# RMSNorm with repeated rows on one NeuronCore: wide squares and reductions, roots on GpSimd, and copies shared with GpSimd

## The chip, the cores and the metric

The kernel runs on one NeuronCore of a Trainium2 chip. The metric is the device time of one execution in microseconds (us), and smaller is better. Four parts of the core matter here: ScalarE (ACT in the profile), VectorE (DVE), GpSimd (POOL), and SyncE (SP), which computes nothing but issues transfers to the core's 16 DMA engines. TensorE does no work in this kernel.

## What is computed

The input `x` has 8 x 512 = 4096 rows of 2048 float32 values. Each row is divided by its root mean square, multiplied elementwise by `gamma`, and written twice, in two neighbouring rows of the output. So 33.6 MB are read and 67.1 MB are written.

```python
x_rep = np.repeat(x, 2, axis=1)
rms = np.sqrt((x_rep ** 2).mean(axis=-1, keepdims=True) + 1e-6)
return (x_rep / rms * gamma[None, None, :]).astype(np.float32)
```

## The kernel before

**Tiles.** The 4096 rows are cut into 8 tiles of 128 partitions x K = 4 rows. A tile `y` in SBUF has 8 row slots of 2048 values in each partition, 64 KB. The load puts the four input rows into slots 4 to 7 (`K * (R - 1) + k`, with R = 2). The result of row k goes to slot 2k, and its copy to slot 2k + 1. So the output overwrites the input row by row, and the whole tile is stored in one piece of 8.4 MB (L55 to L59). The pool `rows` has three such buffers (L39): tile 3 takes the buffer of tile 0, tile 4 that of tile 1, and so on. A load into a buffer has to wait until the store that reads this buffer has landed.

**Work on one row.** ScalarE squares the row and sums it in one pass, with the squares themselves thrown away into PSUM (L64, `accum_out`), and takes the root of the mean (L68). VectorE takes the reciprocal (L73) and computes x times this number times gamma in one instruction, `scalar_tensor_tensor` (L74). It has two tensors as inputs: the row and `gamma_b`, which holds gamma in all 128 partitions.

**Work on one tile** (`compute`, L83). Four times the row work; then ScalarE copies the results of rows 0 and 1 into their second slots and VectorE does so for rows 2 and 3 (L81). Then the store is issued.

**What sets the order.** The schedule is written by hand: each engine works through its instructions in program order. All loads and stores stand in one queue, that of SyncE, and SyncE issues them strictly in this order: load 0 (in two halves), load 1, load 2, store 0, store 1, store 2, load 3, load 4, load 5, store 3, store 4, load 6, load 7, store 5, store 6, store 7 (L91, L99, L100 and the loop at L106 with `loads_after`). Each store waits for its tile's copies, each later load for the store of the tile that had its buffer. While SyncE waits for one of them, nothing that stands behind it can be issued.

**At the start** gamma is fetched in seven pieces on ScalarE's own queue into partition 0 of `gamma_b` (L95), and GpSimd spreads it over the partitions (L96). GpSimd does nothing else.

Of the kernel before, what the change touches and what calls it, by code (L numbers as in the profile page):

```python
# [1 line left out]

# [4 lines left out]


@with_exitstack
def kernel(  # L10
    ctx: ExitStack,
    tc: tile.TileContext,
    x: bass.AP,
    gamma: bass.AP,
    out: bass.AP,
):
    nc = tc.nc
    P = nc.NUM_PARTITIONS
    f32 = mybir.dt.float32
    Act = mybir.ActivationFunctionType  # L20
    Alu = mybir.AluOpType

    B, S, D = x.shape
    Bo, So, Do = out.shape
    R = So // S
    assert R == 2 and D == Do and B == Bo and So == S * R
    eps = 1e-6
    inv_d = 1.0 / float(D)


    K = 4
    N = B * S
    assert N % (P * K) == 0
    ntiles = N // (P * K)
    x_t = x.rearrange("b s d -> (b s) d").rearrange("(n p k) d -> n p k d", p=P, k=K)
    out_t = out.rearrange("b s d -> (b s) d").rearrange("(n p j) d -> n p (j d)", p=P, j=K * R)

    singles = ctx.enter_context(tc.tile_pool(name="singles", bufs=1))
    rows = ctx.enter_context(tc.tile_pool(name="rows", bufs=3))  # L39
    junk = ctx.enter_context(tc.tile_pool(name="junk", bufs=1, space=bass.MemoryType.PSUM))  # L40
    small = ctx.enter_context(tc.tile_pool(name="small", bufs=8))

    ys = []

    def load(i, eng, parts=1):


        y = rows.tile([P, K * R, D], f32, name="y")
        step = K // parts
        for k in range(0, K, step):  # L50
            at = K * (R - 1) + k
            eng.dma_start(out=y[:, at : at + step, :], in_=x_t[i, :, k : k + step, :])
        ys.append(y)

    def store(i, k0, k1):  # L55
        nc.sync.dma_start(  # L56
            out=out_t[i, :, R * k0 * D : R * k1 * D],
            in_=ys[i][:, R * k0 : R * k1, :].rearrange("p j d -> p (j d)"),
        )  # L59

    def square(i, k):
        sq = junk.tile([P, D], f32, name="sq")
        ss = small.tile([P, 1], f32, name="ss")
        nc.scalar.activation(  # L64
            out=sq[:], in_=ys[i][:, K * (R - 1) + k, :], func=Act.Square, accum_out=ss[:]
        )
        rms = small.tile([P, 1], f32, name="rms")
        nc.scalar.activation(out=rms[:], in_=ss[:], func=Act.Sqrt, scale=inv_d, bias=eps_t[:])  # L68
        return rms

    def scale(i, k, rms):
        rstd = small.tile([P, 1], f32, name="rstd")
        nc.vector.reciprocal(out=rstd[:], in_=rms[:])  # L73
        nc.vector.scalar_tensor_tensor(  # L74
            out=ys[i][:, R * k, :], in0=ys[i][:, K * (R - 1) + k, :], scalar=rstd[:], in1=gamma_b[:],
            op0=Alu.mult, op1=Alu.mult,
        )

    def repeat(i, k0, k1, copy):
        y_r = ys[i].rearrange("p (k r) d -> p k r d", r=R)  # L80
        copy(out=y_r[:, k0:k1, 1, :], in_=y_r[:, k0:k1, 0, :])  # L81

    def compute(i):  # L83
        for k in range(K):
            scale(i, k, square(i, k))
        repeat(i, 0, K // 2, nc.scalar.copy)
        repeat(i, K // 2, K, nc.vector.tensor_copy)


    ctx.enter_context(tc.manual_schedule())  # L90
    load(0, nc.sync, parts=2)  # L91
    gamma_b = singles.tile([P, D], f32, name="gamma_b")
    cuts = [0, *range(D // 4, D + 1, D // 8)]
    for c0, c1 in zip(cuts, cuts[1:]):
        nc.scalar.dma_start(out=gamma_b[0:1, c0:c1], in_=gamma[c0:c1].partition_broadcast(1))  # L95
    nc.gpsimd.partition_broadcast(out_ap=gamma_b[:], in_ap=gamma_b[0:1, :])  # L96
    eps_t = singles.tile([P, 1], f32, name="eps_t")
    nc.vector.memset(eps_t, eps)  # L98
    load(1, nc.sync)  # L99
    load(2, nc.sync)  # L100

    assert ntiles == 8
    loads_after = {2: (3, 4, 5), 4: (6, 7)}
    for i in range(ntiles):  # L106
        compute(i)
        store(i, 0, K)
        for j in loads_after.get(i, ()):
            load(j, nc.sync)  # L110


# [1 line left out]
_INS = ['x', 'gamma']  # L114
_OUTS = [((8, 1024, 2048), 'float32')]


# [23 lines left out]
```

## Time and profile before

| | |
|---|---|
| median of 3 runs | 239.39 us (239.35 to 239.60) |
| the profiled execution: its time, its span | 239.72 us, 237.9 us |
| VectorE busy | 96.5 us in 73 instructions (41% of the span) |
| ScalarE busy | 101.0 us in 106 instructions (42%) |
| GpSimd busy | 2.5 us in 5 instructions (1%) |
| moved by DMA | 100.69 MB, 423 GB/s over the span |

The span runs from the first to the last instruction of the profiled execution. The execution's own time is 1.8 us longer, for what lies around the span. "Busy" of an engine counts its computing instructions; waiting and the issuing of transfers do not count. The profile names an instruction by its source line, so "L74" is line 74 of the code above. In the strips with 40 digits each digit stands for 5.9 us and gives the busy share in tenths, with 9 for 90% or more.

### The profile page before, as it was taken

Reading aid. Unit: us, or ns where it says so; the run is one execution under the profiler, and the core shown is the slowest. Engines: PE = TensorE matmul, PEld = TensorE weight load, DVE = VectorE, ACT = ScalarE, POOL = GpSimd, SP = SyncE. Lnnn points to the kernel's source line nnn. Section 1 sums busy time; section 2 is a strip of 40 time slices with the busy share of each in tenths; the row PEclk is TensorE's granted clock in tenths of the full one; section 3 lists DMA queues with packets and bytes.
Section 4 is the critical chain, followed back from the end, with each engine's and each line's share of the span. In section 5 each row is a group of like instructions: output and inputs, shape, how many; then the busy total and the mean of one; then the engine's idle time right before and its main releaser. Section 6 shows DMA issues by size and latency. Waiting matters only on the chain.

```text
span 237.9 us, 287 instructions
## 1 busy us (share of the span) xinstructions
DVE 96.5 (41%) x73; ACT 101.0 (42%) x106; POOL 2.5 (1%) x5
## 2 busy tenths in 40 slices
DVE  0049999960000000059999960000199990000000
ACT  2697999900000000099999920000599960000000
POOL 0030000000000000000000000000000000000000
DMA  7999998989899998999998999989998989999994
GB/s 265 436 446 441 441 441 353 530 353 496 386 452 430 397 485 353 441 441 441 441 518 364 464 419 430 452 369 430 435 518 364 518 364 485 397 452 430 408 474 176
DMA packets 2464, 100.69 MB, mean 423 GB/s; under 512 B 279, under 2 KB 285, under 8 KB 286
## 3 DMA queue, kind: packets, MB, share of 16 engines
q1 hardware_dynamic: 2448, 100.66, 98.5%
q14 instruction: 2, 0.02, 0.0%
q10 hardware_dynamic: 14, 0.01, 0.0%
HBM read 33.56 MB, written 67.11 MB: 423 GB/s over the span
## 4 chain that ended last, share of the span: by engine, by line
DMA 58%; ACT 12%; DVE 9%; issue 1%; POOLq 1%; ACTq 1%; SPq 0%
DMA y<-in_x_dram 33%; DMA out_dram<-y 21%; ACT sq L64 8%; DVE y L74 7%; DMA gamma_b<-in_gamma_dram 4%; ACT y L81 3%; DVE y L81 2%; ACT rms L68 1%; POOLq L136 1%; ACTq L95 1%; DVE rstd L73 0%; POOLq L96 0%; SPq L56 0%
## 5 line engine op out<-in xcount | busy, mean ns | idle before, releaser
L64 ACT ACTIVATE sq<-y 128x2048 f32<-128x2048 f32 x32 | 59.7, 1865 | 87.8 <-DMA y<-in_x_dram 87.8
L74 DVE SCALAR_TENSOR_TENSOR y<-y,rstd,gamma_b 128x2048 f32<-128x2048 f32 x32 | 75.3, 2352 | 4.1 <-POOL gamma_b L96 3.0
L73 DVE RECIPROCAL rstd<-rms 128x1 f32<-128x1 f32 x32 | 5.0, 158 | 94.6 <-ACT rms L68 94.3
L81 ACT COPY y<-y 128x4096 f32<-128x4096 f32 x8 | 28.7, 3590 | 1.4 <-DVE y L74 1.4
L81 DVE COPY y<-y 128x4096 f32<-128x4096 f32 x8 | 18.3, 2294 | 0.3
L68 ACT ACTIVATE rms<-ss,eps_t 128x1 f32<-128x1 f32 x32 | 9.4, 295 | 1.0
L64 ACT ACTIVATION_READ_ACCUMULATOR sq<-y 128x1 f32 x32 | 6.0, 187 | 0.0
L64 ACT ACT_TABLE_LOAD x1 | 1.3, 1283 | 3.0 <-issue 3.0
L96 POOL PARTITION_BROADCAST gamma_b<-gamma_b x1 | 2.3, 2294 | 12.2 <-DMA y<-in_x_dram 12.2
L68 ACT ACT_TABLE_LOAD x1 | 1.3, 1283 | 0.0
L98 DVE MEMSET eps_t<- 128x1 f32 x1 | 0.1, 59 | 0.8 <-PEq L125 0.8
L125 POOL MEMSET const-uint8-127<- 128x1 uint8 x1 | 0.1, 102 | 0.0
L125 POOL MEMSET const-bfloat16-1.0<- 128x1 bf16 x1 | 0.1, 101 | 0.0
L125 POOL MEMSET const-float32-0.0<- 128x1 f32 x1 | 0.1, 98 | 0.2 <-issue 0.2
L125 POOL MEMSET const-float32-1.0<- 128x1 f32 x1 | 0.1, 98 | 0.0
## 6 DMA issues: line engine op xcount, KB each, us to landing
y<-in_x_dram SPq DMA_DIRECT2D x7, 4096.0 KB, 14.6
y<-in_x_dram SPq DMA_DIRECT2D x2, 2048.0 KB, 7.4
out_dram<-y SPq DMA_DIRECT2D x8, 24.4
gamma_b<-in_gamma_dram ACTq DMA_DIRECT2D x6, 1.0 KB
gamma_b<-in_gamma_dram ACTq DMA_DIRECT2D x1, 2.0 KB
```

Source lines behind the costliest of these rows:

```text
L64: nc.scalar.activation(out=sq[:], in_=ys[i][:, K * (R - 1) + k, :], func=Act.Square, accum_out=ss[:])
L68: nc.scalar.activation(out=rms[:], in_=ss[:], func=Act.Sqrt, scale=inv_d, bias=eps_t[:])
L73: nc.vector.reciprocal(out=rstd[:], in_=rms[:])
L74: nc.vector.scalar_tensor_tensor(out=ys[i][:, R * k, :], in0=ys[i][:, K * (R - 1) + k, :], scalar=rstd[:], in1=gamma_b[:], op0=Alu.mult, o ...
L81: copy(out=y_r[:, k0:k1, 1, :], in_=y_r[:, k0:k1, 0, :])
L95: nc.scalar.dma_start(out=gamma_b[0:1, c0:c1], in_=gamma[c0:c1].partition_broadcast(1))
L96: nc.gpsimd.partition_broadcast(out_ap=gamma_b[:], in_ap=gamma_b[0:1, :])
L98: nc.vector.memset(eps_t, eps)
L125: nc = _bacc.Bacc("TRN2", target_bir_lowering=False, num_devices=1)
L136: with _tile.TileContext(nc) as tc:
```

## The change

- **Start.** Gamma's seven pieces are issued by SyncE, five 1 KB pieces and one of 2 KB between the two halves of load 0 and the last one after them, into a small tile `gamma_row` of its own (two halves, in partitions 0 and 32). GpSimd spreads each half by itself. The constants are set by GpSimd, and ScalarE's table for the root is loaded ahead.
- **Tiles 0 and 3** (`by_rows`): squares and sums row by row on ScalarE as before, but one root and one reciprocal for two rows. Copies as before.
- **Tiles 1, 2, 4, 6 and 7** (`mixed`): ScalarE squares the last rows of the tile in one wide instruction (three rows of tiles 1, 2 and 6, two of tile 4, four of tile 7) into slots of the tile that are free until the results come, and VectorE sums them in one wide `tensor_reduce`. The first rows (none for tile 7, one for tiles 1, 2 and 6, two for tile 4) are squared and summed by ScalarE as before. GpSimd turns the sums into reciprocal roots with two small instructions on 128 x 4 values, a `tensor_scalar` and a power of -0.5 (`root`). VectorE scales four rows as before.
- **Copies.** Rows 0 and 1 are copied by GpSimd for tiles 2, 6 and 7 and by ScalarE for tiles 1 and 4. Rows 2 and 3 are copied by VectorE, except in tile 6, where ScalarE does it.
- **Tile 5**: four wide rows of squares (done ahead, during tile 4), one `tensor_reduce`, the root on GpSimd, then ScalarE multiplies each row by its reciprocal root, VectorE multiplies all four rows by gamma in one `tensor_tensor`, and ScalarE copies all four rows. The squares of tile 7 are likewise done ahead, during tile 6.

The order of the loads and stores in SyncE's queue is that of before, apart from gamma's pieces. Their sizes are the same.

As built, the order on VectorE for tile 2 is reduce, four scales, copy; for tile 6 reduce and four scales, followed at once by tile 7's reduce, four scales and copy. On ScalarE the copy of tile 1 stands before the squares of tile 2. GpSimd's copies stand between the roots of their own tile and of the next.

```diff
--- before.py
+++ after.py
@@ -42,72 +42,159 @@
     ys = []
-    def load(i, eng, parts=1):
-        y = rows.tile([P, K * R, D], f32, name="y")
-        step = K // parts
-        for k in range(0, K, step):
-            at = K * (R - 1) + k
-            eng.dma_start(out=y[:, at : at + step, :], in_=x_t[i, :, k : k + step, :])
-        ys.append(y)
-    def store(i, k0, k1):
+    def new_tile():
+        ys.append(rows.tile([P, K * R, D], f32, name="y"))
+    def load(i, k0, k1):
         nc.sync.dma_start(
-            out=out_t[i, :, R * k0 * D : R * k1 * D],
-            in_=ys[i][:, R * k0 : R * k1, :].rearrange("p j d -> p (j d)"),
-        )
-    def square(i, k):
+            out=ys[i][:, K * (R - 1) + k0 : K * (R - 1) + k1, :], in_=x_t[i, :, k0:k1, :]
+        )
+    def store(i):
+        nc.sync.dma_start(out=out_t[i], in_=ys[i].rearrange("p j d -> p (j d)"))
+    H = K // 2
+    x_at = K * (R - 1)
+    def total(i, k, ss):
         sq = junk.tile([P, D], f32, name="sq")
-        ss = small.tile([P, 1], f32, name="ss")
         nc.scalar.activation(
-            out=sq[:], in_=ys[i][:, K * (R - 1) + k, :], func=Act.Square, accum_out=ss[:]
-        )
-        rms = small.tile([P, 1], f32, name="rms")
-        nc.scalar.activation(out=rms[:], in_=ss[:], func=Act.Sqrt, scale=inv_d, bias=eps_t[:])
-        return rms
-    def scale(i, k, rms):
-        rstd = small.tile([P, 1], f32, name="rstd")
-        nc.vector.reciprocal(out=rstd[:], in_=rms[:])
-        nc.vector.scalar_tensor_tensor(
-            out=ys[i][:, R * k, :], in0=ys[i][:, K * (R - 1) + k, :], scalar=rstd[:], in1=gamma_b[:],
-            op0=Alu.mult, op1=Alu.mult,
-        )
-    def repeat(i, k0, k1, copy):
+            out=sq[:], in_=ys[i][:, x_at + k, :], func=Act.Square, accum_out=ss[:, k : k + 1]
+        )
+    def square(i, k0, k1):
+        nc.scalar.activation(
+            out=ys[i][:, k0:k1, :], in_=ys[i][:, x_at + k0 : x_at + k1, :], func=Act.Square
+        )
+    def reduce(i, k0, k1, ss):
+        nc.vector.tensor_reduce(
+            out=ss[:, k0:k1], in_=ys[i][:, k0:k1, :], op=Alu.add, axis=mybir.AxisListType.X
+        )
+    def root(k0, k1, ss):
+        at = ss[:, k0:k1]
+        nc.gpsimd.tensor_scalar(
+            out=at, in0=at, scalar1=inv_d, scalar2=eps, op0=Alu.mult, op1=Alu.add
+        )
+        nc.gpsimd.tensor_tensor(out=at, in0=at, in1=power_t[:, k0:k1], op=Alu.pow)
+    def scale(i, k0, k1, rstd):
+        for k in range(k0, k1):
+            nc.vector.scalar_tensor_tensor(
+                out=ys[i][:, R * k, :], in0=ys[i][:, x_at + k, :], scalar=rstd[:, k : k + 1],
+                in1=gamma_b[:], op0=Alu.mult, op1=Alu.mult,
+            )
+    def repeat(i, k0, k1, copy=nc.scalar.copy):
         y_r = ys[i].rearrange("p (k r) d -> p k r d", r=R)
         copy(out=y_r[:, k0:k1, 1, :], in_=y_r[:, k0:k1, 0, :])
-    def compute(i):
-        for k in range(K):
-            scale(i, k, square(i, k))
-        repeat(i, 0, K // 2, nc.scalar.copy)
-        repeat(i, K // 2, K, nc.vector.tensor_copy)
+    def columns():
+        return small.tile([P, K], f32, name="ss")
     ctx.enter_context(tc.manual_schedule())
-    load(0, nc.sync, parts=2)
+    assert ntiles == 8
     gamma_b = singles.tile([P, D], f32, name="gamma_b")
     cuts = [0, *range(D // 4, D + 1, D // 8)]
-    for c0, c1 in zip(cuts, cuts[1:]):
-        nc.scalar.dma_start(out=gamma_b[0:1, c0:c1], in_=gamma[c0:c1].partition_broadcast(1))
-    nc.gpsimd.partition_broadcast(out_ap=gamma_b[:], in_ap=gamma_b[0:1, :])
+    for _ in range(3):
+        new_tile()
+    gamma_row = singles.tile([64, D // 2], f32, name="gamma_row")
+    def gamma_half(c):
+        at = 32 * (c // (D // 2))
+        return gamma_row[at : at + 1, :]
+    def gamma_piece(c0, c1):
+        at = c0 % (D // 2)
+        nc.sync.dma_start(
+            out=gamma_half(c0)[:, at : at + c1 - c0], in_=gamma[c0:c1].partition_broadcast(1)
+        )
+    power_t = singles.tile([P, K], f32, name="power_t")
+    nc.gpsimd.memset(power_t, -0.5)
     eps_t = singles.tile([P, 1], f32, name="eps_t")
-    nc.vector.memset(eps_t, eps)
-    load(1, nc.sync)
-    load(2, nc.sync)
-    assert ntiles == 8
-    loads_after = {2: (3, 4, 5), 4: (6, 7)}
-    for i in range(ntiles):
-        compute(i)
-        store(i, 0, K)
-        for j in loads_after.get(i, ()):
-            load(j, nc.sync)
+    nc.gpsimd.memset(eps_t, eps)
+    nc.scalar.preload_act_table(Act.Sqrt)
+    load(0, 0, H)
+    for c0, c1 in zip(cuts[:-2], cuts[1:-1]):
+        gamma_piece(c0, c1)
+    load(0, H, K)
+    gamma_piece(cuts[-2], cuts[-1])
+    for c0 in (0, D // 2):
+        nc.gpsimd.partition_broadcast(out_ap=gamma_b[:, c0 : c0 + D // 2], in_ap=gamma_half(c0))
+    load(1, 0, K)
+    load(2, 0, K)
+    def root_quick(k0, k1, ss):
+        at = ss[:, k0:k1]
+        nc.scalar.activation(out=at, in_=at, func=Act.Sqrt, scale=inv_d, bias=eps_t[:])
+        nc.vector.reciprocal(out=at, in_=at)
+    def by_rows(i):
+        ss = [columns() for _ in range(R)]
+        for h, k0 in enumerate(range(0, K, H)):
+            for k in range(k0, k0 + H):
+                total(i, k, ss[h])
+            root_quick(k0, k0 + H, ss[h])
+            scale(i, k0, k0 + H, ss[h])
+        repeat(i, 0, H)
+        repeat(i, H, K, nc.vector.tensor_copy)
+        store(i)
+    def mixed(i, by_row, ahead=None, first=nc.gpsimd.tensor_copy, last=nc.vector.tensor_copy):
+        ss = columns()
+        if by_row:
+            square(i, by_row, K)
+        for k in range(by_row):
+            total(i, k, ss)
+        reduce(i, by_row, K, ss)
+        root(0, K, ss)
+        if ahead is not None:
+            square(*ahead)
+        scale(i, 0, K, ss)
+        repeat(i, 0, H, first)
+        repeat(i, H, K, last)
+        store(i)
+    by_rows(0)
+    mixed(1, 1, first=nc.scalar.copy)
+    mixed(2, 1)
+    for j in (3, 4, 5):
+        new_tile()
+        load(j, 0, K)
+    by_rows(3)
+    mixed(4, H, ahead=(5, 0, K), first=nc.scalar.copy)
+    for j in (6, 7):
+        new_tile()
+        load(j, 0, K)
+    ss = columns()
+    reduce(5, 0, K, ss)
+    root(0, K, ss)
+    for k in range(K):
+        nc.scalar.activation(
+            out=ys[5][:, R * k, :], in_=ys[5][:, x_at + k, :], func=Act.Copy, scale=ss[:, k : k + 1]
+        )
+    y_r = ys[5].rearrange("p (k r) d -> p k r d", r=R)
+    nc.vector.tensor_tensor(
+        out=y_r[:, :, 0, :], in0=y_r[:, :, 0, :],
+        in1=gamma_b[:].rearrange("p (k d) -> p k d", k=1).to_broadcast([P, K, D]), op=Alu.mult,
+    )
+    repeat(5, 0, K)
+    store(5)
+    mixed(6, 1, ahead=(7, 0, K), last=nc.scalar.copy)
+    mixed(7, 0)
 # ---- launch: one core; inputs and outputs as the reference has them ----
```

## The prediction

> **What bounds the kernel now.** I read the page's strips and queue table first, then the groups by cost, then SyncE's waits, the chain that ended last, and the times at which SyncE issued single transfers.
>
> ```profile
> DVE  0049999960000000059999960000199990000000
> ACT  2697999900000000099999920000599960000000
> DMA  7999998989899998999998999989998989999994
> ...
> q1 hardware_dynamic: 2448, 100.66, 98.5%
> ...
> L64 ACT ACTIVATE sq<-y 128x2048 f32<-128x2048 f32 x32 | 59.7, 1865 | 87.8 <-DMA y<-in_x_dram 87.8
> L74 DVE SCALAR_TENSOR_TENSOR y<-y,rstd,gamma_b 128x2048 f32<-128x2048 f32 x32 | 75.3, 2352 | 4.1 <-POOL gamma_b L96 3.0
> ...
> L81 ACT COPY y<-y 128x4096 f32<-128x4096 f32 x8 | 28.7, 3590 | 1.4 <-DVE y L74 1.4
> L81 DVE COPY y<-y 128x4096 f32<-128x4096 f32 x8 | 18.3, 2294 | 0.3
> ...
> L96 POOL PARTITION_BROADCAST gamma_b<-gamma_b x1 | 2.3, 2294 | 12.2 <-DMA y<-in_x_dram 12.2
> ...
> y<-in_x_dram SPq DMA_DIRECT2D x2, 2048.0 KB, 7.4
> ```
>
> (`q1` is SyncE's queue; behind the bar stand busy us, mean ns of one, and the idle time before.) The DMA strip is full from start to end, at 98.5% of 16 engines, while VectorE and ScalarE work in three bursts with long rests. The change moves the same bytes in the same order, so it cannot shorten the middle. It can only lengthen it, where a store is issued after the DMA engines have run dry. SyncE issues in order, so what stands behind a late store is late too.
>
> ```profile
> SPq L56 <- DVE y L81: 108.8, 7, 23.9
> SPq L52 <- DMA out_dram<-y: 69.6, 5, 19.1
> ```
> ```profile
> 27.05 25.77 DMA out_dram<-y
> 52.82 0.02 issue
> 52.84 48.32 DMA y<-in_x_dram
> ...
> 115.86 24.36 DMA out_dram<-y
> 140.22 0.02 issue
> 140.24 29.08 DMA y<-in_x_dram
> 169.32 0.02 issue
> ```
> ```profile
> 72.14 0.34 SPq L52 DMA_DIRECT2D y<-in_x_dram  x1
> ```
> ```profile
> 91.56 0.33 SPq L52 DMA_DIRECT2D y<-in_x_dram  x1
> ```
>
> Each of the two waits is in the order of things: stores wait for VectorE's copy, then loads for a store to land. In the chain the first column is the start. Store 0 lands at 52.82 us, and loads 4 and 5, which wait for stores 1 and 2, go out at 72.14 and 91.56. So a store takes 19.4 us of the DMA engines' time and a load half, 9.7. Load 6 lands at 169.3, load 7 therefore at 179.0, stores 5, 6 and 7 at 198.4, 217.8 and 237.2, which fits the span's end at 237.9.
>
> How early must a transfer be issued? The first half of load 0 took 7.4 us from issue to landing, alone. Its 2.1 MB are a quarter of a store: 4.8 us. The other 2.6 us lie before the first and after the last byte. So a transfer leaves no hole if it is issued 2.6 us before its predecessor lands. That gives **deadlines**: store 0 30.8, store 1 50.2, store 2 69.5, store 3 about 118 (load 5 lands at 101.2 + 2 x 9.7), store 4 137.6, store 5 176.4, store 6 195.8, store 7 215.2. Before, the stores went out at 27.0, 39.2, 51.4, 115.9, 128.2, 160.1, 184.0 and 196.4: every one in time, mostly by far.
>
> **What the skill says.** (1) "SBUF — State Buffer", section "Who interferes with whom": GpSimd has no SBUF ports of its own but shares a pair with VectorE. A VectorE instruction with two inputs in SBUF contends with a GpSimd instruction that reads SBUF, a copy in the two-port mode contends in any case, and the loser waits for the whole instruction; `tensor_reduce` never contends. The trace before cannot confirm this, since GpSimd is idle after 15 us. VectorE's copy, 4096 values in 2.29 us against 2.35 us for 2048 in L74, shows the doubled rate. (2) "VectorE: DVE Perf Modes", tier table: `tensor_reduce` has only the single rate; no row here shows it. (3) "DMA: Bandwidth & Descriptors", section "Issuing engines are not separate DMA queues": all queues share the 16 engines, so gamma's move to SyncE saves no transfer time. The strip agrees.
>
> **The prices.** A wide square follows from ScalarE's 1.87 us for 2048 and 3.59 for 4096: 5.3 us for three rows, 7.0 for four. L74's 2.35 us are 2.13 at 0.96 values per ns (the VectorE page's clock) and 0.22 fixed, so a reduction takes 4.5 us for two rows, 6.6 for three, 8.75 for four. Two unknowns:
> - **r, the root on GpSimd.** GpSimd's memsets take 0.1 us each and a handover 0.03, so at least 0.3. The power has no row and no price; I allow 3. I take 1.0, as two short instructions of some tenths each with two handovers.
> - **c, GpSimd's copy of two rows.** "GPSIMD Engine Reference", section 3, gives 1.03 cycles per element for simple bodies and 1.8 for a tight loop, at 1.2 GHz: an estimated 3.5 to 6.1 us. The nearest row, the broadcast of 2048 values in 2.29 us, scales to 4.6. I take 4.0. If it shares the port it adds c to VectorE's work; if not, 0.
>
> **The change part by part.**
>
> *Start.* The two halves of the broadcast cost at least 1.15 us each. The last gamma piece follows the second half of load 0 and lands near 13.0; the first scale then begins near 14.4 (before: 14.9), up to 15.6 if a half costs as much as the whole did. The root table load saved on ScalarE (1.28 us) lies beside this. Four scales at 2.365 us, one reciprocal and the copy end near 26.4: store 0 is 4 us early, so all of this, gain or loss, is worth nothing. Of gamma's seven issues on SyncE (0.3 us each), six lie beside load 0. The last, as built, waits for the first half of load 0 to land (8.1), and loads 1 and 2 behind it go out 0.3 us later than before, while load 0 keeps the engines busy to about 11 us.
>
> *Tile 1.* ScalarE copies tile 0 until 22.7, squares three rows until 28.0. Reduce to 34.7, root, four scales of 9.5 us in sum, copy: 46.5 + r. Store 1 goes out at 47.5, in time by 2.7.
>
> *Tile 2.* ScalarE's copy of tile 1 waits for two scales (39.4 + r), so tile 2's squares end at 48.4 + r. Reduce 6.6: 55.0 + r. Root, four scales: 64.5 + 2r. VectorE's copy: 66.8 + 2r, which is 68.8, still in time by 0.7. But GpSimd's copy becomes ready after the second scale, and from there scales 3 and 4 (two inputs), VectorE's copy (two ports) and GpSimd's copy all need the shared port. In whatever order they go, the last ends at 66.8 + 2r + c = 72.8. Deadline 69.5: **3.3 us of idle DMA**, with load 3 queued behind store 2. From here on everything moves with the DMA, and I go on in the old times.
>
> *Tile 3.* Load 3 lands at 101.15. Two totals, root, two scales, two more, copy: store 3 at 117.7 instead of 115.9 (the first scale waits for a second total, 2.0). Deadline 118: just in time.
>
> *Tile 4.* Reduce 117.75 to 122.25, root, scales and copy: 134.0 + r, deadline 137.6. The squares of tile 5 delay only ScalarE's copy, which ends at 132.4. *Tile 5.* 135 + 8.75 + r, four scaled copies on ScalarE (7.6), the product (8.75), the copy of four rows (7.0): 168.1, deadline 176.4. Nothing.
>
> *Tile 6.* Squares 169.3 to 174.65, reduce to 181.3, root, two scales: 187.0. The third scale, queued right behind, takes the port first, to 189.4. GpSimd's copy is then waiting and gets it, to 193.4; the fourth scale ends at 195.75 and ScalarE's copy behind it at 199.35. Deadline 195.8: **3.55 us**. The squares of tile 7, which stand ahead of that copy on ScalarE and wait for load 7, end at 186.0 and delay nothing.
>
> *Tile 7.* Reduce 195.75 to 204.5, root, two scales: 210.25. Two scales (4.7), VectorE's copy (2.3) and GpSimd's copy (4.0) on one port: 221.3. The root of tile 7 stands behind tile 6's copy on GpSimd, which is done at 193.4. Deadline 215.2 + 3.55 = 218.75: **2.55 us**.
>
> Sum: 3.3 + 3.55 + 2.55 = 9.4 us. The span goes from 237.9 to 247.3 and the profiled execution from 239.72 to 249.1; on the median, 0.33 us lower, **248.8**. In letters the sum is 4r + 3c - 6.6.
>
> **Rivals.**
> - *VectorE keeps the port*: the fourth scale starts before GpSimd is served, and GpSimd copies tile 6 during tile 7's reduction. Tile 6 is then in time (195.75) and tile 7 2.1 late: 3.3 + 2.1 = 5.4, so 244.8. For it: 0.03 us between two scales in the trace. Against it: a waiting request.
> - *No contention between the scales and GpSimd* (the side of no change). Both inputs of a scale would go through VectorE's own ports or share without loss, and c lies beside scales 3 and 4 (4.7 us). Then stores 2, 6 and 7 are due at 68.8, 195.4 and 213.3, all in time, and the DMA hides everything: 239.4. It decides as soon as the time that GpSimd adds in tile 2 is under 0.7 us. For it: the trace shows no contention, having no such pair.
> - *The power is slow*: r = 3 without contention. Tile 2 is late by 3.3, tile 6 by 1.6, tile 7 by 0.5: 244.8. For it: no row prices it.
> - *Faster*: only the 1.5 us before the first packet and the end could give something, and neither is touched.
>
> **How the numbers follow.** My case 0.43, VectorE keeps the port 0.2, no contention 0.24, slow power 0.08, others (faster by a little among them) 0.05. My case alone runs from r = 0.5, c = 3.5 (245.3) to c = 4.6 with r = 1.6 (253). No contention must be inside the range, so it goes from 239.2 to 253. About 0.2% can be told from no change. Of no contention 0.19 falls within that, 0.05 above it, where tile 3 or the root uses up its small margin. Faster 0.04, same 0.19, slower 0.77.
>
> **What would show it.** In the changed kernel's trace: GpSimd's three copies beside scales of more than 2.35 us or gaps before them; holes in the DMA strip near 70, 200 and 220 us and none near 30, 50 or 120; store 2 issued near 73; ScalarE's late copy in tile 6. The prediction is wrong if scales run at 2.35 us back to back beside GpSimd's copy, if the power takes several us, or if a hole appears at tile 3 or at the start.

## The result, and the profile after

| | before | after |
|---|---|---|
| median (lowest to highest, runs) | 239.50 us (239.29 to 239.90, 6) | 247.84 us (247.76 to 248.11, 6) |
| ratio after / before | | 1.0348, 95% interval 1.0335 to 1.0361 |
| the profiled execution: its time, its span | 239.72, 237.9 us | 248.0, 246.1 us |
| time that the DMA packets took (share of q1 x span) | 98.5% x 237.9 = 234.3 us | 96.1% x 246.1 = 236.5 us |
| rest of the span | 3.6 us | 9.6 us |

The changed kernel is slower by 8.3 us. The page of the changed kernel: the strips, the queue, and the groups that stand for the lines shown of before and for the new operations.

```profile
DVE  0059689977990000019979990490097997994000
ACT  2677901950000000088999107509949050000000
POOL 0220010001620000000010001000001801270000
DMA  7999999899949796999998979799999779797793
...
q1 hardware_dynamic: 2462, 100.67, 96.1%
...
L87 DVE SCALAR_TENSOR_TENSOR y<-y,ss,gamma_b 128x2048 f32<-128x2048 f32 x28 | 74.4, 2694 | 10.0 <-POOL ss L83 7.5
L74 DVE TENSOR_REDUCE ss<-y 128x3 f32<-128x6144 f32 (+2 forms) x6 | 41.4, 6905 | 17.0 <-ACT y L69 17.0
L63 ACT ACTIVATE sq<-y 128x2048 f32<-128x2048 f32 x13 | 24.4, 1874 | 60.1 <-DMA y<-in_x_dram 59.9
L94 ACT COPY y<-y 128x4096 f32<-128x4096 f32 (+1 forms) x6 | 25.0, 4172 | 30.8 <-DVE y L87 22.1
...
L94 POOL COPY y<-y 128x4096 f32<-128x4096 f32 x3 | 16.9, 5634 | 14.2 <-DVE y L87 14.2
...
L94 DVE COPY y<-y 128x4096 f32<-128x4096 f32 x6 | 13.8, 2293 | 0.2
...
L83 POOL TENSOR_TENSOR ss<-ss,power_t 128x4 f32<-128x4 f32 x6 | 6.1, 1017 | 0.5
L131 POOL PARTITION_BROADCAST gamma_b<-gamma_row x2 | 2.6, 1301 | 11.7 <-DMA gamma_row<-in_gamma_dram 11.7
```

And SyncE's waits (total, times, longest):

```profile
SPq L56 <- DVE y L94: 127.1, 6, 25.9
SPq L51 <- DMA out_dram<-y: 43.7, 3, 19.9
SPq L56 <- ACT y L94: 38.3, 2, 29.6
```

In the DMA strip the 4 in the twelfth slice (68 to 74 us) is new: there the queue was empty. The 6s and 7s after it can't be read by themselves, since a slice beside a 9 can be low only because long packets are counted where they start; the finer windows below decide. The waits show the same shift: SyncE waits 43.7 us for stores to land, before 69.6, and longer for computed tiles (127.1 + 38.3 against 108.8 for VectorE's copies). The chain that ended last reaches back over the last 6% of the span only and is of no use here. The mean scale has grown from 2352 to 2694 ns, but all the growth is in three instructions, one for each tile that GpSimd copies, as the view of `y` shows for tile 2 (shortest, median and longest in ns, then first and last start):

```profile
L87 DVE SCALAR_TENSOR_TENSOR y<-y,ss,gamma_b x4: 2347/2350/5565, 59.0 to 65.9; 128x2048 f32<-128x2048 f32 x4
```

The timeline of tile 2 in the changed kernel (start, duration, instruction, idle time of its engine before it):

```profile
50.92 6.55 DVE L74 TENSOR_REDUCE ss<-y 128x3 f32<-128x6144 f32 x1 [1.98 <-ACT y L69]
57.64 0.20 POOL L80 TENSOR_SCALAR ss<-ss 128x4 f32<-128x4 f32 x1 [20.32 <-DVE ss L74]
57.92 1.01 POOL L83 TENSOR_TENSOR ss<-ss,power_t 128x4 f32<-128x4 f32 x1
58.97 12.48 DVE L87 SCALAR_TENSOR_TENSOR y<-y,ss,gamma_b 128x2048 f32<-128x2048 f32 x4 [1.49 <-POOL ss L83]
63.65 5.65 POOL L94 COPY y<-y 128x4096 f32<-128x4096 f32 x1 [4.72 <-DVE y L87]
71.48 2.29 DVE L94 COPY y<-y 128x4096 f32<-128x4096 f32 x1
73.90 0.33 SPq L56 DMA_DIRECT2D out_dram<-y  x1
74.33 1.34 SPq L51 DMA_DIRECT2D y<-in_x_dram  x2
```

The reduction ends at 57.47 and the first scale starts at 58.97: the way over GpSimd and back costs 1.5 us. GpSimd's copy becomes ready at 63.65, beside the third scale (2.35 us). The fourth starts at 65.88, as if nothing were in the way, but lasts 5.57 us: it waits for the copy, which ends at 69.30.

```profile
65.88 5.57 DVE L87 SCALAR_TENSOR_TENSOR y<-y,ss,gamma_b 128x2048 f32<-128x2048 f32 x1
```

Store 2 goes out at 73.90 and load 3 only behind it. The DMA in windows of 1 us at tile 2 and tile 6 (busy time and count of VectorE, ScalarE and GpSimd, the clock, then the DMA share and GB/s):

```profile
70.00:71.00 1.00, 1.00 (x1) 0.00 (x0) 0.00 (x0) 1.00 0.60 262
71.00:72.00 1.00, 0.97 (x2) 0.00 (x0) 0.00 (x0) 1.00 0.01 0
72.00:73.00 1.00, 1.00 (x1) 0.00 (x0) 0.00 (x0) 1.00 0.00 0
73.00:74.00 1.00, 0.77 (x1) 0.00 (x0) 0.00 (x0) 1.00 0.00 0
74.00:75.00 1.00, 0.00 (x0) 0.00 (x0) 0.00 (x0) 1.00 2.50 1049
201.00:202.00 1.00, 1.00 (x1) 1.00 (x1) 0.00 (x0) 1.00 0.00 0
202.00:203.00 1.00, 1.00 (x1) 1.00 (x1) 0.00 (x0) 1.00 0.01 0
203.00:204.00 1.00, 1.00 (x1) 0.01 (x1) 0.00 (x0) 1.00 1.84 786
```

Next to nothing starts while store 2 and store 6 are awaited. (A share above 1 in a window, such as 2.50, can only come from packets that run on beyond it.) Followed packet by packet, the trace has holes of 2.95 us before store 2, 1.82 before store 6 and 1.71 before store 7 (means over the 16 engines, so that packets still under way are counted), and none elsewhere: **6.5 us**. The packets themselves took **2.2 us** longer than before (236.5 against 234.3). The 16 engines finish together, whereas before their mean finished 0.8 us ahead of the last: **-0.8 us**. That makes 7.9 of the span's 8.2; most of the rest lies between the last packet and the end of the span (1.5 us, before 1.2).

### The profile page after: what moved, and what is told of

It is laid out like the page before. It is cut to its first block, busy times and chain, and to the rows that moved or that the text cites. A ratio compares the mean times of both kernels' runs of the same rounds, so it can differ in the third digit from the quotient of the medians.

```text
span 246.1 us, 233 instructions
## 1 busy us (share of the span) xinstructions
DVE 138.6 (56%) x45; ACT 94.0 (38%) x47; POOL 27.1 (11%) x23
## 3 DMA queue, kind: packets, MB, share of 16 engines
q1 hardware_dynamic: 2462, 100.67, 96.1%
## 5 line engine op out<-in xcount | busy, mean ns | idle before, releaser
L87 DVE SCALAR_TENSOR_TENSOR y<-y,ss,gamma_b 128x2048 f32<-128x2048 f32 x28 | 74.4, 2694 | 10.0 <-POOL ss L83 7.5
L74 DVE TENSOR_REDUCE ss<-y 128x3 f32<-128x6144 f32 (+2 forms) x6 | 41.4, 6905 | 17.0 <-ACT y L69 17.0
L63 ACT ACTIVATE sq<-y 128x2048 f32<-128x2048 f32 x13 | 24.4, 1874 | 60.1 <-DMA y<-in_x_dram 59.9
L94 ACT COPY y<-y 128x4096 f32<-128x4096 f32 (+1 forms) x6 | 25.0, 4172 | 30.8 <-DVE y L87 22.1
L69 ACT ACTIVATE y<-y 128x6144 f32<-128x6144 f32 (+2 forms) x6 | 33.6, 5605 | 3.9 <-DMA y<-in_x_dram 3.9
L94 POOL COPY y<-y 128x4096 f32<-128x4096 f32 x3 | 16.9, 5634 | 14.2 <-DVE y L87 14.2
L190 DVE TENSOR_TENSOR y<-y,gamma_b 128x8192 f32<-128x8192 f32 x1 | 8.7, 8693 | 9.3 <-ACT y L186 9.3
L94 DVE COPY y<-y 128x4096 f32<-128x4096 f32 x6 | 13.8, 2293 | 0.2
L186 ACT ACTIVATE y<-y,ss 128x2048 f32<-128x2048 f32 x4 | 7.8, 1995 | 13.2 <-POOL ss L83 13.2
L83 POOL TENSOR_TENSOR ss<-ss,power_t 128x4 f32<-128x4 f32 x6 | 6.1, 1017 | 0.5
```

Source lines behind the costliest of these rows:

```text
L63: nc.scalar.activation(out=sq[:], in_=ys[i][:, x_at + k, :], func=Act.Square, accum_out=ss[:, k : k + 1])
L69: nc.scalar.activation(out=ys[i][:, k0:k1, :], in_=ys[i][:, x_at + k0 : x_at + k1, :], func=Act.Square)
L74: nc.vector.tensor_reduce(out=ss[:, k0:k1], in_=ys[i][:, k0:k1, :], op=Alu.add, axis=mybir.AxisListType.X)
L83: nc.gpsimd.tensor_tensor(out=at, in0=at, in1=power_t[:, k0:k1], op=Alu.pow)
L87: nc.vector.scalar_tensor_tensor(out=ys[i][:, R * k, :], in0=ys[i][:, x_at + k, :], scalar=rstd[:, k : k + 1], in1=gamma_b[:], op0=Alu.mul ...
L186: nc.scalar.activation(out=ys[5][:, R * k, :], in_=ys[5][:, x_at + k, :], func=Act.Copy, scale=ss[:, k : k + 1])
```

## The experiments

My theory after the result was that of the prediction. GpSimd's copy takes the port that a scale needs, the roots lie in the path, and the DMA runs dry three times. Rivals were that wide instructions or the copies cost time by themselves, that the start costs something, and that the packets are slower for a reason unconnected with the holes. "Packets" and "rest" are worked out for each run as in the table above.

| run | median, us | ratio, 95% interval | span | packets | rest |
|---|---|---|---|---|---|
| no_pool_copy | 243.42 | 1.0170 (1.0141 to 1.0199) | 241.1 | 236.5 | 4.6 |
| pool_copy_alone | 239.44 | 1.0001 (0.9992 to 1.0009) | 237.5 | 234.4 | 3.1 |
| gamma_psum | 242.86 | 1.0132 (1.0109 to 1.0156) | 241.9 | 237.1 | 4.8 |
| pool_memset | 242.79 | 1.0143 (1.0124 to 1.0162) | 241.0 | 237.1 | 3.9 |
| swap_halves | 243.75 | 1.0183 (1.0120 to 1.0245) | 242.0 | 237.4 | 4.6 |
| quick_roots | 242.84 | 1.0140 (1.0124 to 1.0156) | 240.9 | 236.1 | 4.8 |
| no_pool_quick | 240.28 | 1.0034 (1.0019 to 1.0049) | 238.7 | 235.1 | 3.6 |
| roots_alone | 242.75 | 1.0145 (1.0128 to 1.0162) | 240.8 | 236.5 | 4.3 |
| start_alone | 239.56 | 1.0003 (0.9995 to 1.0012) | 237.8 | 234.5 | 3.3 |
| load3_first | 245.59 | 1.0268 (1.0230 to 1.0306) | 243.5 | 235.2 | 8.3 |
| late_store | 245.85 | 1.0275 (1.0260 to 1.0290) | 243.9 | 236.1 | 7.8 |
| repaired | 239.52 | 1.0012 (1.0002 to 1.0022) | 237.6 | 234.3 | 3.3 |

**no_pool_copy**: the changed kernel with ScalarE in place of GpSimd for the copies of tiles 2, 6 and 7.

```diff
-    mixed(2, 1)
+    mixed(2, 1, first=nc.scalar.copy)
...
-    mixed(6, 1, ahead=(7, 0, K), last=nc.scalar.copy)
-    mixed(7, 0)
+    mixed(6, 1, ahead=(7, 0, K), first=nc.scalar.copy, last=nc.scalar.copy)
+    mixed(7, 0, first=nc.scalar.copy)
```

> The changed kernel, with GpSimd's three copies (rows 0 and 1 of tiles 2, 6 and 7) given to ScalarE. Port theory (a scale with two SBUF inputs and GpSimd's copy can't run together, which adds about 3.2 us to tiles 2, 6 and 7 each): all scales take 2.35 us or less, store 2 goes out at about 70.7 us, 1 us late, stores 6 and 7 are in time: about 240.4 us. Root-and-reduction theory (the longer chain on VectorE and GpSimd's roots make the loss, the copies lie beside it): 245 us or more.

All scales take 2.35 us again (9.26 for tile 2's four), and store 2 goes out at 70.68, 3.2 us earlier. The holes are gone but for 0.13 us. Yet the time falls by 4.4 us only, to 3 us above what I expected: the packets still take 236.5 us. So the port is one cause, and there is a second, which is no hole.

**pool_copy_alone**: the kernel before, with GpSimd copying rows 0 and 1 of tiles 2, 6 and 7.

```diff
-        repeat(i, 0, K // 2, nc.scalar.copy)
+        repeat(i, 0, K // 2, nc.gpsimd.tensor_copy if i in (2, 6, 7) else nc.scalar.copy)
```

> The kernel before, with only one part of the change: rows 0 and 1 of tiles 2, 6 and 7 are copied by GpSimd. Port theory: one scale in each of these tiles takes about 5.6 us instead of 2.35, but the stores have 11 us and more to spare, so nothing is lost: 239.5 us. Theory that GpSimd's copying slows the DMA or the kernel as such: 2 to 3 us per copy, 245 us or more.

The port is lost in the same way (tile 2's third scale takes 5.70 us, since here GpSimd was first), and store 2 goes out at 54.55 instead of 51.4. Its deadline is 15 us later, so nothing is lost. The contention costs something only where the store is late.

**gamma_psum**: the changed kernel, but the scales of tiles 2, 6 and 7 read gamma from PSUM, where ScalarE put a copy during tile 1. GpSimd's copies stay.

```diff
+    fixed = ctx.enter_context(tc.tile_pool(name="fixed", bufs=1, space=bass.MemoryType.PSUM))
...
-                in1=gamma_b[:], op0=Alu.mult, op1=Alu.mult,
+                in1=gamma_p[:] if i in (2, 6, 7) else gamma_b[:], op0=Alu.mult, op1=Alu.mult,
...
+        if i == 1:
+            nc.scalar.copy(out=gamma_p[:], in_=gamma_b[:])
```

> The changed kernel, with gamma for the scales of tiles 2, 6 and 7 read from PSUM (ScalarE puts a copy there while it is idle in tile 1). GpSimd's copies stay. Port theory: a scale has only one SBUF input, so no scale is stretched, GpSimd's copies run beside scales 3 and 4 and take 3.3 to 3.6 us as the trace shows them, and the time is that without GpSimd's copies, about 240.5 us. Theory that GpSimd's copy disturbs VectorE whatever it reads, or that roots and reductions make the loss: about 247.8 us.

Its timeline of tile 2:

```profile
59.24 9.25 DVE L88 SCALAR_TENSOR_TENSOR y<-y,ss,gamma_p 128x2048 f32<-128x2048 f32 x4 [1.48 <-POOL ss L84]
63.91 3.60 POOL L95 COPY y<-y 128x4096 f32<-128x4096 f32 x1 [4.71 <-DVE y L88]
```

With one input in SBUF the scales run as if alone, 9.25 us for four against 12.48, and the copy beside them takes 3.60 us against 5.65. So it is the second SBUF input that meets GpSimd, and the recorded 5.65 us contained some 2 us of waiting. The time is that of no_pool_copy, with the same unexplained 2 to 3 us.

**pool_memset**: the changed kernel with GpSimd writing zeros instead of copying. The copies of rows 0 and 1 of tiles 2, 6 and 7 are left out.

```diff
+    def fill(out, in_):
+        nc.gpsimd.memset(out, 0.0)
...
-    mixed(2, 1)
+    mixed(2, 1, first=fill)
```

(and likewise for tiles 6 and 7)

> The changed kernel, with GpSimd's three copies replaced by memsets of the same destinations: GpSimd then writes and reads nothing (the copies of rows 0 and 1 of tiles 2, 6 and 7 are left out, zeros stand there). If a two-input scale and GpSimd contend for the read side of the shared port only: no scale is stretched, about 243.4 us as without GpSimd's copies. If any GpSimd access to SBUF blocks a two-input scale: one scale per tile is stretched by about the memset's length, 246 to 248 us.

```profile
58.88 3.51 POOL L172 MEMSET y<- 128x4096 f32 x1
58.96 9.27 DVE L87 SCALAR_TENSOR_TENSOR y<-y,ss,gamma_b 128x2048 f32<-128x2048 f32 x4 [1.48 <-POOL ss L83]
```

The memset lies fully beside the scales and stretches none. Writing does not contend, reading does. With gamma_psum this is what the Trainium skill says in "SBUF — State Buffer", section "Who interferes with whom": a VectorE instruction with two SBUF inputs meets a GpSimd instruction that reads SBUF, not one that only writes it.

**swap_halves**: the changed kernel with GpSimd copying rows 2 and 3 of tiles 2, 6 and 7, after all scales, and ScalarE rows 0 and 1.

```diff
-    mixed(2, 1)
+    mixed(2, 1, first=nc.scalar.copy, last=nc.gpsimd.tensor_copy)
```

(and likewise for tiles 6 and 7)

> The changed kernel, with GpSimd copying rows 2 and 3 of tiles 2, 6 and 7 instead of rows 0 and 1, and ScalarE rows 0 and 1. GpSimd then reads only after the last scale of its tile; beside it runs nothing, or tile 7's reduction. Port theory: no scale above 2.35 us, the copy takes 3.6 us as it did beside scales that read PSUM, store 2 goes out near 72.0, 1.3 us after that of the kernel without GpSimd's copies, and the time is 1.3 us above its 243.4: 244.7. Theory that any GpSimd copy beside VectorE's work costs: 247.

The scales are back at 2349 ns and the copy takes 3.60 us at 67.89; store 2 goes out at 71.51, between the two cases, with a hole of 0.7 us. In tile 6 the copy (3.60 us from 195.08) lies beside tile 7's reduction (8.68 us from 194.93), and neither is longer than elsewhere: a reduction doesn't meet a copy. The time is 1 us below the expectation, but its runs spread widely (242.69 to 245.38).

**quick_roots**: the changed kernel with the roots of the mixed tiles and of tile 5 on ScalarE and VectorE; GpSimd's copies stay.

```diff
-        root(0, K, ss)
+        root_quick(0, K, ss)
...
-    root(0, K, ss)
+    root_quick(0, K, ss)
```

> The changed kernel, with the roots of tiles 1, 2, 4, 5, 6 and 7 made by ScalarE's square root and VectorE's reciprocal instead of GpSimd. Port theory with a root of 1.6 us on the path in tiles 1, 2, 6 and 7: the root falls to about 0.55 us, so 4 x 1.05 = 4.2 us come back: 243.6 us. If the roots make the whole loss: 239.5 us. If they cost nothing: 247.8 us.

```profile
55.38 0.30 ACT L142 ACTIVATE ss<-ss,eps_t 128x4 f32<-128x4 f32 x1 [4.79 <-DVE ss L74]
55.71 0.18 DVE L143 RECIPROCAL ss<-ss 128x4 f32<-128x4 f32 x1 [0.42 <-ACT ss L142]
55.92 12.48 DVE L87 SCALAR_TENSOR_TENSOR y<-y,ss,gamma_b 128x2048 f32<-128x2048 f32 x4
```

Its timeline of tile 2 shows the root's new way: the reduction, from 48.73, ends at 55.28, and the first scale starts at 55.92, 0.64 us later instead of 1.5. The scales are stretched as before the edit. In all 5.0 us come back, and the holes shrink to 0.3, 0.8 and 0.9 us. Four roots account for 4 x (1.5 - 0.64) = 3.4 (tiles 1, 2, 6 and 7); the rest is not the path of the roots. The first scale of tile 0, before any root on GpSimd, starts at 14.50 here and at 15.20 in the changed kernel, since load 0 lands earlier.

**no_pool_quick**: both, no copy and no root on GpSimd.

> The changed kernel without GpSimd's copies (ScalarE makes them) and with the roots on ScalarE and VectorE: the wide squares and reductions, tile 5's product and the start remain. Every store is then about 1 us or more ahead of its deadline (store 2 near 68.6). If late stores are the whole loss: 239.5 to 240. If the start or the wide instructions slow the transfers: 241 to 242.

It is 0.8 us slower than before. Store 2 goes out at 67.59, there is no hole, and 0.65 us of slower packets lie between 170 and 190 us. Wide squares, reductions and tile 5 together therefore cost no more than these 0.8 us, whose cause stays open; in the last experiment, which has them too, most of them are not there.

**roots_alone**: the kernel before, with the roots of tiles 1 to 7 on GpSimd, one for each row.

```diff
+            nc.gpsimd.tensor_scalar(
+                out=rstd[:], in0=rms[:], scalar1=inv_d, scalar2=eps, op0=Alu.mult, op1=Alu.add
+            )
+            nc.gpsimd.tensor_tensor(out=rstd[:], in0=rstd[:], in1=power_t[:], op=Alu.pow)
```

> The kernel before, with only the roots of tiles 1 to 7 moved to GpSimd, row by row (28 pairs of a small tensor_scalar and a power). Each pair takes 1.3 us and a row's chain grows by about 1.2 us, but a row every 2.4 us keeps VectorE the slower one, and every store stays far ahead of its deadline: 239.5 us. If GpSimd's roots cost time as such, not only through their place in a chain without slack: 241 us or more.

The expectation was missed by 3.2 us. The timeline of tile 1:

```profile
27.86 2.35 DVE L82 SCALAR_TENSOR_TENSOR y<-y,rstd,gamma_b 128x2048 f32<-128x2048 f32 x1 [0.77 <-POOL rstd L79]
27.91 2.35 POOL L76 TENSOR_SCALAR rstd<-ss 128x1 f32<-128x1 f32 x1
...
30.34 0.55 POOL L79 TENSOR_TENSOR rstd<-rstd,power_t 128x1 f32<-128x1 f32 x1
30.93 2.35 DVE L82 SCALAR_TENSOR_TENSOR y<-y,rstd,gamma_b 128x2048 f32<-128x2048 f32 x1 [0.72 <-POOL rstd L79]
```

GpSimd's instruction on a single value per partition, 0.19 us at its shortest in this run, stands for 2.35 us and ends just after the scale beside it (27.86 to 30.21): it waits for that scale. VectorE's copy holds it up too: the one at 26.14 lasts 1.00 us, until the copy of tile 0 (24.80 to 27.09) is done. So the root of the next row cannot be had during the scale of this one, and a row takes 3.07 us (27.86 to 30.93) instead of 2.46. I had forgotten that the port works in this direction too. Store 3 then goes out at 119.38, with a hole of 0.36 us. The remaining 2.2 us are slower packets, in a kernel without GpSimd copies, wide instructions or the new start.

**start_alone**: the kernel before with the start of the changed one (gamma on SyncE, two broadcasts, constants and table ahead).

> The kernel before, with only the changed start: gamma in seven pieces on SyncE's queue, two half broadcasts, the constants on GpSimd, the root's table loaded ahead. In the changed kernel the holes in the DMA work make about 6 of the 8.3 us, and the packets together took 2.2 us longer (96.1% of 246.1 against 98.5% of 237.9). If gamma's pieces in the loads' queue cause these 2 us: 241 to 241.5. If small margins before the stores cause them: 239.5.

No difference, and packets of 234.5 us: the start by itself, with gamma's pieces between the halves of load 0, is not what slows the packets.

**load3_first**: the changed kernel with load 3 ahead of store 2 in SyncE's queue. Load 3 waits only for store 0.

```diff
-    mixed(2, 1)
-    for j in (3, 4, 5):
+    mixed(2, 1, early=3)
+    for j in (4, 5):
```

(`early` issues that load just before the tile's store)

> The changed kernel, with load 3 ahead of store 2 in SyncE's queue; all computing is as it was, the stretched scale in tile 2 too. Hole theory: load 3 fills the hole near 71 to 74 us, store 2 is no longer awaited by idle DMA engines, and 3 us come back: 244.9. Theory that the stretched scales themselves make the loss: 247.8.

Tile 2 is as slow as before this edit (four scales in 12.48 us, store 2 at 73.59), but the hole near 72 us is gone and 2.3 us come back, 0.7 less than expected. The packets take 1.3 us less than in the changed kernel (235.2 against 236.5), the hole before store 7 stays at 1.7 us, and that before store 6 grows from 1.8 to 3.4: part of what is won at tile 2 is lost again there. So the late compute of tile 2 costs time only because the queue behind it is empty.

**late_store**: the kernel before with row 3 of tile 2 scaled ten more times, so that store 2 is late with neither GpSimd nor wide instructions.

```diff
+        if i == 2:
+            for _ in range(10):
+                nc.vector.scalar_tensor_tensor(
+                    out=ys[i][:, R * 3, :], in0=ys[i][:, K * (R - 1) + 3, :], scalar=last[:],
+                    in1=gamma_b[:], op0=Alu.mult, op1=Alu.mult,
+                )
```

> The kernel before, with ten more scales of tile 2's last row (same inputs, same result) ahead of VectorE's copy, so that store 2 goes out near 74.7 us instead of 51.4; nothing else is changed. Hole theory: the DMA engines have run dry at about 71 us and idle until about 75.4; if only the hole counts, 4.4 us: 243.9. If the loads that follow a hole are also slower, as the lower rate per busy share near 90 to 96 us of the changed kernel suggests, 1 us more: 244.9. If the queue hides a late store: 239.5.

Store 2 goes out at 75.10, the hole is 4.6 us, and the packets take 1.8 us longer (236.1). Packet by packet, 0.86 us of that lie between 86 and 100 us, where store 2 gives way to load 3, and 0.85 between 112 and 130. So a late store costs more than its hole: transfers behind it, where the queue changes between stores and loads, run slower too.

**repaired**: the changed kernel with three edits from above: gamma in PSUM for tiles 2, 6 and 7, roots on ScalarE and VectorE, load 3 ahead of store 2. GpSimd's copies, wide squares and reductions, tile 5 and the start stay.

> The changed kernel with three repairs: gamma from PSUM for the scales of tiles 2, 6 and 7, roots on ScalarE and VectorE, load 3 ahead of store 2 in SyncE's queue. GpSimd's three copies, the wide squares, the reductions and tile 5 stay. Port and hole theory: no scale stretched, no hole: 239.5 to 240.3 us. If the wide instructions or GpSimd's copies carry a cost of their own: 241 us or more.

The page of repaired:

```profile
DMA  6999998989999998999999998989998989989894
...
q1 hardware_dynamic: 2462, 100.67, 98.6%
```

Its median stands 0.12% above the kernel before (interval 0.02 to 0.22%). Five of its 20 runs lie at 240.25 to 240.69 us, above all 23 runs of before that were taken with it (239.15 to 240.04); why stays open, and the profiled run (239.34) isn't one of them. So GpSimd's copies and the wide instructions cost by themselves some 0.2 us on the median, if anything. No version beat the kernel before, whose floor is the transfer of 100.7 MB.

**The second cause.** The slower packets lie in three places. Summed by transfer, the 2.2 us of the changed kernel are 0.6 in loads 0 to 2, 1.1 in store 2 and load 3, and 0.45 in load 7.
- *Out of step from the start.* In the seven kernels that make roots on GpSimd, the last packet of loads 0 to 2 ends between 34.2 and 35.0 us; in the seven without (the kernel before among them) between 32.9 and 33.2. Store 0's first packet starts at 32.4 to 32.5 in all of them, so some of the 16 engines fall up to 2 us and more behind the others. It can be seen at the end of load 0, whose last packet ends at 12.7 to 13.5 us with these roots and at 12.4 to 12.7 without, long before the first power is computed (36.26 us in the changed kernel). Engines that are ahead don't wait, but the end is that of the last one. Why a kernel with these roots loses this time stays open.
- *After a late or nearly late store.* The packets from 90 to 96 us, first in the changed kernel, then in the one before:

```profile
90.00:96.00 6.00, 0.00 (x0) 0.00 (x0) 0.00 (x0) 1.00 0.77 262
```
```profile
90.00:96.00 6.00, 0.00 (x0) 0.00 (x0) 0.00 (x0) 1.00 1.01 437
```

A share of 0.77 moved 262 GB/s, that is 340 for a full share; before it was 437 / 1.01 = 433. At 433, the same bytes would have taken 0.77 x 6 x (1 - 340 / 433) = 1.0 us less. quick_roots and late_store show it without roots on GpSimd; roots_alone and load3_first, which have these roots but don't keep the DMA engines waiting for store 2, don't show it. So it belongs to the late store. It isn't settled what in the DMA engines makes it so.
- *In load 7.* Its packets take 0.45 us more than before in the changed kernel, 0.58 in no_pool_quick and 0.93 in roots_alone, and no more in start_alone and repaired. Neither the roots nor a late store 2 are common to the first three; the cause stays open.

## Why the prediction was right, and where it was not

Predicted were 248.8 us, measured 247.84. The mechanism was right: a full DMA queue, three late stores, at the named tiles. Its terms, one by one:

| step | predicted | measured |
|---|---|---|
| first scale | 14.4 (up to 15.6) | 15.20 |
| reduction of 2, 3, 4 rows | 4.5, 6.6, 8.75 us | 4.42, 6.55, 8.67 |
| wide squares, 3 and 4 rows | 5.3, 7.0 us | 5.32, 7.02 |
| root over GpSimd, r | 1.0 us | 1.5 |
| what GpSimd's copy adds, c | 4.0 us | 3.2 (12.48 - 9.26) |
| store 2 issued | 72.8 | 73.90 |
| hole at tile 2, 6, 7 | 3.3, 3.55, 2.55 | 2.95, 1.82, 1.71 |
| sum of holes | 9.4 us | 6.5 |
| slower packets | none | 2.2 |

- **The bound and the deadlines as an idea: right.** pool_copy_alone has the same stretched scales without loss, load3_first the same late tile without a hole.
- **The size of the deadline: wrong, and the largest error.** The 2.6 us "before the first and after the last byte" came from the first half of load 0, issued into an empty machine, and not "alone": its second half went out 1.3 us behind it (2.03). In the changed kernel store 6 has its first packet at 203.91, 0.84 us after its issue at 203.07; and in the kernel before, load 4 goes out at 72.14, 0.47 us after store 1's last packet (71.67). So about 1.3 us are needed, not 2.6. That makes the holes at tiles 2 and 6 1.3 us too long each, 2.6 us together. At tile 7 the error drops out, since its deadline is counted from the late store 6: the issues of stores 6 and 7 lie 21.12 us apart, and less the 19.4 us of a store that is the measured hole of 1.7.
- **"All of this, gain or loss, is worth nothing" of the start: right for the start, but not for a late load 0.** Without roots on GpSimd the first scale starts at 14.50 (quick_roots), against 14.4 predicted, and the start costs nothing (start_alone). With these roots the loads land later, the first scale starts at 15.20, and ScalarE waits another 0.39 us for load 1 before it squares tile 1, which it doesn't in quick_roots. From there to tile 2 the chain has no slack to make this up: tile 2's reduction starts at 50.92, where the prediction, with the measured r, has 48.4 + 1.5 = 49.9. So 1.0 us of the first hole is the early lag.
- **r and c: both off by less than 1 us, in opposite directions.** 4r + 3c is 16 as predicted and 15.6 as measured. That the roots lie in the path is right: 3.4 us of what quick_roots returns is theirs.
- **The order at the port: right.** One more scale, then GpSimd's copy, then the fourth scale. The rival *VectorE keeps the port* would have shown the fourth scale at 2.35 us; *no contention* falls with the 5.57 us. *The power is slow* falls with r = 1.5, though the early lag comes with the roots on GpSimd.
- **Tiles 1, 3, 4 and 5: right.** Stores 1, 3, 4 and 5 went out at 49.01, 122.00, 139.5 and 173.07, with no hole at any of them.
- **Slower packets: not foreseen.** With the measured r and c and the right deadline, the prediction's sum is 15.6 - 6.6 - 2.6 = 6.4 us; with the 1.0 us of early lag it is 7.4, against 6.5 measured. The 0.9 us that are left are small differences in the chain, the largest at tile 7 (2.25 against 1.71). It would still have missed the 2.2 us of packets. That the total came within 1 us is luck in part: holes that were 2.9 us too long stand against 2.2 us of slower packets that were overlooked.

## What to carry to other kernels

In a kernel that the DMA queue bounds, write down for every transfer the time by which it has to be queued, and weigh a change by the margin it uses up, not by the busy time it saves or adds. In these runs GpSimd was a free helper beside VectorE's reductions and beside scales with one operand in PSUM, and where it only wrote. Beside scales that read two tensors from SBUF, a GpSimd instruction that reads SBUF held VectorE up or was itself held up, until the other's instruction was done. If a store may be late, let a load that is ready stand ahead of it in the queue.

## What the runs showed of the hardware that was not expected

- A GpSimd instruction on one value per partition waits until VectorE's scale beside it is done: 2.35 us for a `tensor_scalar` that takes 0.19 us at its shortest (roots_alone).
- GpSimd's recorded duration contains this wait: 5.65 us for a copy that takes 3.60 us beside scales that read gamma from PSUM (3.51 for a memset of the same size).
- A late store costs its hole and about 0.9 to 1.0 us more where it gives way to the next load (late_store, quick_roots, the changed kernel).
- In the seven kernels with roots on GpSimd, some DMA engines fall 2 us and more behind others during the first loads; the cause is open.
